# A hybrid mLSTM and attention block on one core: the value product copied out of its bank, with first transfers, last store and fifty pieces at other times

## The chip, the cores and the metric

The kernel runs on one core of one Trainium2 chip, as one launch. The metric is the device time of one execution in microseconds. A core has five engines that each work through their own queue in order: TensorE (PE; its weight loads are shown apart as PEld), VectorE (DVE), ScalarE (ACT), GpSimd (POOL) and SyncE (SP), which only issues transfers here. They meet at semaphores. SBUF holds the tiles, PSUM the eight banks that TensorE writes. Transfers are issued on the queues of SP, ACT and POOL and moved by 16 DMA engines.

## The reference

Sequence of 1024 tokens, model width 1024, float32. One layer:

```python
h = rms(x, norm1_g)
p = h @ w_in
qk_m = silu(dwconv_centred(p[..., C_QK_M:C_V_M], conv_w, conv_b))
mix_a = mlstm_group(qk_m, ...)      # 4 heads x 128, forward and backward scans in chunks of 128
mix_b = diff_attention_group(...)   # 4 heads, q and k of 2 x 64, v of 128, blocks of 128 queries
x = x + concat(mix_a, mix_b) @ w_out
u = square(relu(rms(x, norm2_g) @ w_ff1))      # 4096 wide
x = x + u @ w_ff2
```

In the attention, with two logit matrices per head and a bias by distance:

```python
a = softmax(l0) - lam * softmax(l1)
out = rms(a @ v, sub_g) * (1 - lam_init)
```

## The kernel before

**Matmuls.** A float32 product is made of three passes: each operand is cut into a hi part (rounded to the matmul's format, by a ScalarE copy) and a lo part (the rest, by a VectorE or GpSimd subtract), and hi x hi, lo x hi and hi x lo are summed in PSUM. TensorE's rate over these passes is what the rest is arranged around.

**Stages, in order of time.** The value projection (L207 to L254), with the row norms' squares beside it; the key and gate projection; the query projection and norms of the attention; the conv projections with the depthwise convolution (taps L675) and the mLSTM; the attention with 32 items (8 query blocks, 4 heads), with the out-gate and output projections between them; the MLP's first product, in seven block products per pair of column blocks instead of eight (L1404 to L1406); its second product, likewise (L1733 to L1735).

**The start.** Twelve matmuls on a tile of ones (L196) run while the first transfers are under way. The loop over k takes x tile k and half of a weight tile: SP issues, ScalarE cuts hi (`hhi`, L222, scaled by the norm's vector out of `vecs`), VectorE lo (`hlo`, L223). Of k = 0 the x tile comes in four parts of 256 columns, after the first half of w_v; the 24 matmuls (L237) run hi x hi for all eight token tiles first, then lo x hi, then hi x lo. `wstage` and its `load` (L171 to L174) issue the weight load on SP, cut hi on ScalarE and lo on VectorE.

**The one-hot table.** Four transfers `oh` (L383) feed four matmuls that spread the position bias; three buffers. POOL issues the first three at the start of its queue. The rsqrt of the norms is a power on POOL (L89), with the exponent tile `mhalf` (-0.5).

**Planners.** The order of work on the engines from the conv stage on is written by two planners. Each piece of work has a due time in ticks (a tick is a group of projection matmuls) and a running number; `when` adds it to a table, and `moved` holds by running number what is added to a due time. Where the engines' queues get their order, pieces stand sorted by due time; engines run them in that order. The first table has 956 entries (mLSTM and attention), the second 1160 (MLP).

```python
def when(t, f, *args):
    heapq.heappush(table, (t + moved.get(len(made), 0.0), len(made), f, args))
    made.append(t)
```

**Attention.** An item is one query block of one head. Its steps: both logit products (`att_logits`, L970) into two banks `pl`, with bias and minimum on VectorE (L975); exps on ScalarE (L981); the weighted difference on VectorE (L987 to L990); transposes into `pa` (L997) and copies `at` by ScalarE (L1001); the value product into `pav` (L1008). `pav` is one bank for all items, and also holds the transposes `pt` of four items (L1030). After the product ScalarE squares it with a row sum into `on` (L1014), POOL adds the epsilon and takes the rsqrt (L1015, L1016, L89), VectorE scales `pav` into `on` (L1023). Four items on, `on` is transposed and cut into `mix` (ScalarE L1035, VectorE L1039).

**MLP.** In the first product, `m` banks are read by VectorE (L1487, L1492 and others); weights are cut by ScalarE (L1317) and VectorE (L1320). In the second, step i = 4 is last: `finish` subtracts bank n from `zv[n]` (L1779) and `out` stores it (L1748), n = 0 to 3.

**Head turns.** `head_turn` transposes normalised heads into bank `pzTrue` (L352), cuts them (L128 on ScalarE, L360 on VectorE) into tiles of the tag "zz" and stores them.

Of the kernel before, what the change touches and what calls it, by code (L numbers as in the profile page):

```python
# [10 lines left out]
F32 = mybir.dt.float32  # L11
# [5 lines left out]
P = 128  # L17
# [31 lines left out]
def hybrid_block_kernel(ctx: ExitStack, tc: tile.TileContext, xT, w_v, w_kg, w_c, w_va, w_qa, w_o, w_1, w_2, vec, rel, onehot, outT):  # L49
# [26 lines left out]
    nc.sync.dma_start(vecs[:, 0:V_CW], vec[:, 0:V_CW])  # L76
# [9 lines left out]
    nc.gpsimd.memset(mhalf, -0.5)  # L86

    def rsqrt(out, x, n):
        return nc.gpsimd.tensor_tensor(out, x, mhalf[:, 0:n], op=ALU.pow)  # L89
# [101 lines left out]
    with tc.tile_pool(reuse_waits="tile", name="ps0", bufs=8, space=PSUM) as ps0:  # L191
# [16 lines left out]
        for k in range(KT):  # L208

            parts = (4, 2)[k] if k < 2 else 1  # L210
            n = S // parts
            xts[k] = xt = stp.tile([P, S], F32, tag="xt", name=f"xt{k}", bufs=4)
            if k % 2 == 0:
                whi, wlo, wload = wstage(f"v{k}", nc.vector)
            for i in range(parts):
                sl = slice(i * n, (i + 1) * n)
                if k == 0 and i == 0:
                    wload(w_v[0], 0, HB)
                elif k > 1 and k % 2 == 0:
                    wload(w_v[k // 2], 0, 1024)  # L220
                load = nc.sync.dma_start(xt[:, sl], xT[k][:, sl])
                nc.scalar.activation(hhi[k][:, sl], xt[:, sl], AF.Copy, scale=vcol(V_G1 + k))  # L222
                last = nc.vector.scalar_tensor_tensor(  # L223
                    hlo[k][:, sl], xt[:, sl], vcol(V_G1 + k), hhi[k][:, sl].bitcast(F32), op0=ALU.mult, op1=ALU.subtract
                )
                if k == 0 and i == parts - 1:
                    wload(w_v[0], HB, HB)
            if k > 0:
                squares(k - 1)
            if k > 1:  # L230
                last = add_up(k - 1)
            o = (k % 2) * HB
            ops = [(hhi[k], whi), (hlo[k], whi), (hhi[k], wlo)]
            order = [(t, i) for i in range(3) for t in range(NC)] if k == 0 else [(t, i) for t in range(NC) for i in range(3)]
            for t, i in order:
                a, b = ops[i]
                nc.tensor.matmul(  # L237
                    pv[t], a[:, t * P : (t + 1) * P], b[:, o : o + HB], start=k == 0 and i == 0, stop=k == KT - 1 and i == 2
                )
            if k == 2:  # L240
                with tc.issue_after(load.ins):
                    nc.sync.dma_start(vecs[:, V_CW:], vec[:, V_CW:])
            if k == 5:
                with tc.issue_after(last.ins):
                    parameters()
# [33 lines left out]
    def drain():  # L279
# [91 lines left out]
    def distance_bias():  # L371
# [8 lines left out]
        for i in range(4):  # L380
            sl = slice(i * HB, (i + 1) * HB)
            oh = kgp.tile([32, HB], F32R, tag="oh", name=f"oh{i}", bufs=3)
            nc.gpsimd.dma_start(oh, onehot[:, sl])  # L383
# [7 lines left out]

    def first_norms():
# [4 lines left out]
        rsqrt(rcol, rcol, NC)  # L397
# [12 lines left out]
    for t in range(NC):  # L410
# [33 lines left out]
        if t == 4:  # L444
            pending.append(head_turn(kgp, "zz", 3, zs[0], 0, False))
# [122 lines left out]
    pending.append(head_turn(kgp, "zz", 3, zs[1], 1, False))  # L568
# [3 lines left out]
    def qa_done(t, p):  # L572
        head_norm(kgp, p[:, None, :], (zs[2] if t < 4 else z1)[:, t % 4], t, "q")
        if t == 4:
            pending.append(distance_bias())
            pending.append(head_turn(kgp, "zz", 3, zs[2], 0, True))
# [433 lines left out]
    def att_square(it):  # L1010
# [3 lines left out]
        nc.scalar.activation(it.on, it.pav[:, 0:P], AF.Square, accum_out=sm[:, 5:6])  # L1014
# [6 lines left out]
    def att_unit(it):  # L1021

        nc.vector.tensor_scalar(it.on, it.pav[:, 0:P], it.sm[:, 7:8], None, op0=ALU.mult)  # L1023
# [341 lines left out]
    for j in range(4):  # L1365
# [383 lines left out]

    zx, zv = {}, {}  # L1750
# [32 lines left out]
    for s, (i, j) in enumerate(steps):  # L1783
# [23 lines left out]
        if j == NJ - 1:  # L1807
            for n in range(4):
                f = t + 2.01 + 1.5 + 2 * n if i != 4 else t + 0.5 * (n + 1) + 0.01
                when(f, finish, i, n)  # L1810
# [83 lines left out]
```

## Time and profile before

| | us |
|---|---|
| runs | 1248.34, 1248.34, 1248.42 |
| median | 1248.34 |
| profiled execution, its own time | 1248.9 |
| profiled execution, span | 1247.1 |
| TensorE idle in the span | 12.3 |
| granted TensorE clock | 1.00 |

The page lists busy time per engine, the chain of work that ended last, and groups of instructions by line. In a timeline a row gives the start, the duration, engine, line, operation, what it writes and reads and how many instructions follow one another; in square brackets how long the engine was idle before and which engine and line ended that. A row of the waits names the waiting engine and line, the line it waited for, the sum, the count and the longest. Rows of windows give, per stretch, busy time and instructions of PE, PEld, DVE, ACT and POOL, then the granted clock, the DMA share and GB/s. A matmul of 512 columns is shown with some 0.39 us but the next starts some 0.23 us after it, since they are pipelined.

### The profile page before, as it was taken

Reading aid. Unit: us, or ns where it says so; the run is one execution under the profiler, and the core shown is the slowest. Engines: PE = TensorE matmul, PEld = TensorE weight load, DVE = VectorE, ACT = ScalarE, POOL = GpSimd, SP = SyncE. Lnnn points to the kernel's source line nnn. Section 1 sums busy time; section 2 is a strip of 40 time slices with the busy share of each in tenths; the row PEclk is TensorE's granted clock in tenths of the full one; section 3 lists DMA queues with packets and bytes.
Section 4 is the critical chain, followed back from the end, with each engine's and each line's share of the span. In section 5 each row is a group of like instructions: output and inputs, shape, how many; then the busy total and the mean of one; then the engine's idle time right before and its main releaser. Section 6 shows DMA issues by size and latency. Waiting matters only on the chain.

```text
span 1247.1 us, 17168 instructions
## 1 busy us (share of the span) xinstructions
PE 1234.8 (99%) x6443; PEld 1032.4 (83%) x6443; DVE 824.0 (66%) x1138; ACT 622.1 (50%) x1069; POOL 235.0 (19%) x260
## 2 busy tenths in 40 slices
PE   9999999999999989999999999999999999999998
PEld 7898778888878878888887888888888888888887
DVE  7435558885357787774879886666645774568754
ACT  7223437777446576665456454544534443333332
POOL 0033404464324363422000000000000000004001
PEclk9999999999999999999999999999999999999999
DMA  7404254454275486535544764444359746445732
GB/s 249 152 19 169 45 187 112 112 144 136 82 242 175 158 276 196 166 102 204 176 161 144 269 210 170 156 140 169 134 183 357 265 167 195 136 129 172 223 110 93
DMA packets 101458, 208.31 MB, mean 167 GB/s; under 512 B 8688, under 2 KB 21744, under 8 KB 101376
## 3 DMA queue, kind: packets, MB, share of 16 engines
q1 hardware_dynamic: 78368, 154.50, 38.8%
q10 hardware_dynamic: 15008, 31.50, 6.7%
q0 software_dynamic: 8000, 21.24, 5.3%
q8 instruction: 50, 0.82, 0.3%
q14 instruction: 32, 0.26, 0.1%
HBM read 148.90 MB, written 58.29 MB: 166 GB/s over the span
## 4 chain that ended last, share of the span: by engine, by line
PE 88%; DVE 4%; DMA 2%; POOL 2%; issue 2%; ACT 1%; SPq 0%; ACTq 0%; POOLq 0%; DVEq 0%
PE z L1735 8%; PE z L1733 8%; PE z L1734 8%; PE m L1404 7%; PE m L1405 7%; PE m L1406 7%; PE pav L1008 5%; PE pl L970 4%; PE pv L237 3%; PE pw L138 3%; PE pw L140 2%; PE pw L139 2%; PE pa L997 2%; PE pj_c L138 1%; PE po L138 1%
## 5 line engine op out<-in xcount | busy, mean ns | idle before, releaser
L1771 POOL TENSOR_TENSOR zx<-zx,res 128x512 f32<-128x512 f32 x4 | 8.7, 2179 | 491.5 <-DVE zx L1769 491.5
L1735 PE MATMUL z<-wbh,wa0l 128*128 128x512 f32 x224 | 87.4, 390 | 0.1
L975 DVE CUSTOM_DVE_ANT_0 l<-pl,toe 128x1024 f32<-128x1024 f32 x64 | 76.3, 1222 | 16.7 <-PE pl L970 15.6
L1735 PE MATMUL z<-weh,wa1l 128*128 128x512 f32 x224 | 87.2, 389 | 0.0
L1733 PE MATMUL z<-wbh,wa0h 128*128 128x512 f32 x224 | 87.2, 389 | 0.0
L1734 PE MATMUL z<-wel,wa1h 128*128 128x512 f32 x224 | 87.1, 389 | 0.0
L1734 PE MATMUL z<-wbl,wa0h 128*128 128x512 f32 x224 | 87.1, 389 | 0.0
L1733 PE MATMUL z<-weh,wa1h 128*128 128x512 f32 x224 | 87.1, 389 | 0.0
L1317 ACT ACTIVATE weh<-g 128x1024 fp32r<-128x1024 f32 x28 | 29.7, 1061 | 90.5 <-PE z L1735 53.4
L1317 ACT ACTIVATE wbh<-g 128x1024 fp32r<-128x1024 f32 x28 | 29.7, 1061 | 89.9 <-PE z L1735 53.0
L981 ACT ACTIVATE l<-l,sm 128x1024 f32<-128x1024 f32 x64 | 73.1, 1148 | 1.1 <-DVE sm L975 1.1
L1320 DVE TENSOR_TENSOR wel<-g,weh 128x1024 fp32r<-128x1024 f32 x28 | 35.2, 1258 | 56.8 <-ACT weh L1317 56.8
L1453 ACT ACTIVATE sq<-sq 128x512 f32<-128x512 f32 x48 | 30.3, 630 | 81.5 <-DVE sq L1492 65.4
L1320 DVE TENSOR_TENSOR wbl<-g,wbh 128x1024 fp32r<-128x1024 f32 x28 | 35.4, 1264 | 53.2 <-ACT wbh L1317 53.2
L1008 PEld LDWEIGHTS pav<-v,at 128*128 128x128 f32 x512 | 61.5, 191 | 6.5 <-ACT l L981 1.9
L1008 PE MATMUL pav<-v,at 128*128 128x128 f32 x512 | 62.8, 276 | 2.7 <-DVE on L1023 1.5
L138 PE MATMUL pj_c<-hhi,w_c 128*128 128x512 f32 x128 | 53.3, 417 | 0.0
L970 PE MATMUL pl<-kk,q 64*128 64x512 f32 x384 | 53.3, 409 | 0.0
L138 PE MATMUL pw<-mix,hi_wo 128*128 128x512 f32 x128 | 52.0, 406 | 0.0
L140 PE MATMUL pj_c<-hhi,w_c 128*128 128x512 f32 x128 | 50.4, 394 | 0.0
L1735 PEld LDWEIGHTS z<-wbh,wa0l 128*128 128x128 f32 x224 | 42.1, 188 | 9.7 <-DVE wa0l L1320 0.8
L140 PE MATMUL pw<-mix,lo_wo 128*128 128x512 f32 x128 | 50.0, 391 | 0.0
(454 smaller groups left out, 3606.1 us busy)
## 6 DMA issues: line engine op xcount, KB each, us to landing
g<-g_dram SPq DMA_DIRECT2D x56, 512.0 KB, 4.5
g_dram<-gs SPq DMA_DIRECT2D x64, 256.0 KB, 4.5
g_dram<-sq ACTq DMA_DIRECT2D x42, 256.0 KB, 2.0
kk<-k_dram POOLq DMA_DIRECT2D x16, 512.0 KB, 6.2
raw_wo<-in_w_o_dram SPq DMA_DIRECT2D x16, 512.0 KB, 5.0
re<-in_w_dram SPq DMA_DIRECT2D x16, 512.0 KB, 4.3
ro<-in_w_dram SPq DMA_DIRECT2D x16, 512.0 KB, 3.7
zt<-in_w_dram SPq DMA_DIRECT2D x16, 512.0 KB, 4.3
```

Of the source, the lines that this page charges most:

```text
L138: nc.tensor.matmul(out, ahi, bhi, start=start, stop=False)
L140: latest[0] = nc.tensor.matmul(out, alo, bhi, start=False, stop=stop).ins
L970: nc.tensor.matmul(it.pl[x][:, sl], hd.q[r, i, qi * P : (qi + 1) * P], hd.kk[r, j, sl], start=n == 0, stop=n == 2)
L975: nc.vector.tensor_tensor_reduce(lt, it.pl[m], hd.toe[:, off : off + S], 1.0, 3.0e38, ALU.add, ALU.min, it.sm[:, m : m + 1])
L981: nc.scalar.activation(lt, lt, AF.Exp, bias=sm[:, m : m + 1], scale=-1.0, accum_out=sm[:, 2 + m : 3 + m])
L1008: nc.tensor.matmul(it.pav[:, 0:P], at, it.head.v[:, c], start=c == 0, stop=c == NC - 1)
L1404: nc.tensor.matmul(p, wh, xh, start=go, stop=False, skip_group_check=True)
L1405: nc.tensor.matmul(p, wh, xl, start=False, stop=False, skip_group_check=True)
L1406: nc.tensor.matmul(p, wl, xh, start=False, stop=stop and k == 3, skip_group_check=True)
L1733: nc.tensor.matmul(p, wh, gh, start=go, stop=False, skip_group_check=True)
L1734: nc.tensor.matmul(p, wh, gl, start=False, stop=False, skip_group_check=True)
L1735: nc.tensor.matmul(p, wl, gh, start=False, stop=end, skip_group_check=True)
```

## The change

Six places change.

- **Start.** The first half of w_v is issued on ScalarE's queue and its hi copy made by VectorE; x tile 0 comes in two halves, the norm's vectors behind the first of them, the second half of w_v behind the second (cut by ScalarE). The 24 matmuls of k = 0 go by halves of the token tiles: hi x hi, lo x hi, hi x lo for tiles 0 to 3, then for 4 to 7. `mhalf` is made by ScalarE.
- **One-hot.** The four `oh` issues stand behind the rsqrt of the first row norms on POOL.
- **Head turns.** The tag "zz" has four buffers instead of three.
- **Attention.** ScalarE first copies `pav` into `on` in SBUF; the square reads this copy and writes a tile of its own, `osq` (one buffer); VectorE's scaling reads `on` and writes `on`.
- **Last store.** The last subtract of 128x512 is made in two halves of 256 columns, each stored at once, the first on ScalarE's queue and the second on SP's.
- **Fifty due times,** 33 in the first planner's table and 17 in the second's, are changed or added; many of them change the order on no engine.

```diff
-    nc.sync.dma_start(vecs[:, 0:V_CW], vec[:, 0:V_CW])
...
-    nc.gpsimd.memset(mhalf, -0.5)
...
-            parts = (4, 2)[k] if k < 2 else 1
+            parts = 2 if k < 2 else 1
...
+            if k == 0:
+
+                whi, wlo, raw_v = w_tiles("v0")
+                nc.scalar.dma_start(raw_v[:, 0:HB], w_v[0][:, 0:HB])
+
+                nc.scalar.activation(mhalf, ones[:, 0:16], AF.Copy, scale=-0.5)
+                nc.vector.tensor_copy(whi[:, 0:HB], raw_v[:, 0:HB])
...
+                load = nc.sync.dma_start(xt[:, sl], xT[k][:, sl])
                 if k == 0 and i == 0:
+                    nc.sync.dma_start(vecs[:, 0:V_CW], vec[:, 0:V_CW])
...
+                if k == 0:
+
+                    h = slice(i * HB, (i + 1) * HB)
+                    if i == 1:
+                        nc.sync.dma_start(raw_v[:, h], w_v[0][:, h])
+                        nc.scalar.activation(whi[:, h], raw_v[:, h], AF.Copy)
+                    nc.vector.tensor_tensor(wlo[:, h], raw_v[:, h], whi[:, h].bitcast(F32), op=ALU.subtract)
...
-            order = [(t, i) for i in range(3) for t in range(NC)] if k == 0 else [(t, i) for t in range(NC) for i in range(3)]
+            order = [(t, i) for t in range(NC) for i in range(3)]
+            if k == 0:
+                order = [(t, i) for h in range(2) for i in range(3) for t in range(4 * h, 4 * h + 4)]
...
-            nc.gpsimd.dma_start(oh, onehot[:, sl])
+            with tc.issue_after(rooted[0]):
+                nc.gpsimd.dma_start(oh, onehot[:, sl])
...
-        rsqrt(rcol, rcol, NC)
+        rooted[0] = rsqrt(rcol, rcol, NC).ins
...
-            pending.append(head_turn(kgp, "zz", 3, zs[2], 0, True))
+            pending.append(head_turn(kgp, "zz", 4, zs[2], 0, True))
...
-        nc.scalar.activation(it.on, it.pav[:, 0:P], AF.Square, accum_out=sm[:, 5:6])
+
+        nc.scalar.activation(it.on, it.pav[:, 0:P], AF.Copy)
+        sq = tpool.tile([P, P], F32, tag="osq", name=f"osq{it.qb}{it.h}", bufs=1)
+        nc.scalar.activation(sq, it.on, AF.Square, accum_out=sm[:, 5:6])
...
-        nc.vector.tensor_scalar(it.on, it.pav[:, 0:P], it.sm[:, 7:8], None, op0=ALU.mult)
+        nc.vector.tensor_scalar(it.on, it.on, it.sm[:, 7:8], None, op0=ALU.mult)
...
+    def last_out():
+
+        for q, eng in enumerate((nc.scalar, nc.sync)):
+            sl = slice(q * 256, (q + 1) * 256)
+            nc.vector.tensor_tensor(zv[3][:, sl], zv[3][:, sl], banks[3][:, sl], op=sub)
+            eng.dma_start(outT[7][:, sl], zv[3][:, sl])
...
+                if i == 4 and n == 3:
+                    when(f, last_out)
+                    continue
```

Of the due times, those on which the prediction's steps rest (first table: 35 and 36 are the transposes of a head turn in the conv stage, 583 to 585 square, root and unit of one item of the attention; the second table's 403 to 447 lie about the first blocks of the MLP's first product):

```diff
-        1: 0.691, 20: 0.16, 22: 0.093, 25: -2.784, 36: 4.667, 37: 1.04, 43: -0.133, 92: 2.944, 95: 2.082,
+        1: 0.691, 5: -0.831, 20: 0.16, 22: 0.093, 25: -2.985, 35: 0.788, 36: 6.729, 37: 1.04, 43: -0.133, 52: 0.273,
...
-        576: -0.046, 577: 0.164, 582: 0.308, 583: 0.177, 584: 0.168, 585: 0.062, 586: 0.272, 589: 0.199, 590: 0.004,
+        577: 0.276, 582: 0.308, 583: 0.23, 584: 0.221, 585: 0.114, 586: 0.409, 589: 0.199, 590: 0.141, 592: -0.206,
...
-        147: -0.499, 159: -0.024, 403: 0.444, 404: 0.722, 405: 0.71, 406: 0.304, 417: -0.257, 418: -0.02,
-        446: -0.049, 478: 0.543, 581: 0.182, 600: 0.109, 654: 0.417, 655: 0.138, 656: 0.274, 663: 0.859, 668: 0.021,
+        138: 0.131, 139: -0.54, 147: -0.499, 159: -0.024, 403: 0.38, 404: 0.864, 405: 0.765, 406: 0.353, 407: 0.004,
+        417: -0.257, 418: 0.728, 419: 0.029, 420: 0.02, 436: 0.469, 446: -0.049, 447: -0.63, 464: 0.362, 478: 0.543,
```

More of the change, by code (lines that the diff above doesn't have):

```diff
@@ L208, in hybrid_block_kernel @@
         for k in range(KT):
-            parts = (4, 2)[k] if k < 2 else 1
+            parts = 2 if k < 2 else 1
             n = S // parts
             xts[k] = xt = stp.tile([P, S], F32, tag="xt", name=f"xt{k}", bufs=4)
-            if k % 2 == 0:
+            if k == 0:
[3 more added lines that the diff above has]
+                nc.vector.tensor_copy(whi[:, 0:HB], raw_v[:, 0:HB])
+            elif k % 2 == 0:
                 whi, wlo, wload = wstage(f"v{k}", nc.vector)
+                wload(w_v[k // 2], 0, 1024)
             for i in range(parts):
                 sl = slice(i * n, (i + 1) * n)
+                load = nc.sync.dma_start(xt[:, sl], xT[k][:, sl])
                 if k == 0 and i == 0:
[L218 to L221, printed above, removed]
+                    nc.sync.dma_start(vecs[:, 0:V_CW], vec[:, 0:V_CW])
                 nc.scalar.activation(hhi[k][:, sl], xt[:, sl], AF.Copy, scale=vcol(V_G1 + k))
@@ L225, in hybrid_block_kernel @@
                 )
-                if k == 0 and i == parts - 1:
-                    wload(w_v[0], HB, HB)
+                if k == 0:
[4 more added lines that the diff above has]
+                    nc.vector.tensor_tensor(wlo[:, h], raw_v[:, h], whi[:, h].bitcast(F32), op=ALU.subtract)
             if k > 0:
@@ L390, in distance_bias @@
             yield
+    rooted = [None]
     def first_norms():
@@ L444, in hybrid_block_kernel @@
         if t == 4:
-            pending.append(head_turn(kgp, "zz", 3, zs[0], 0, False))
+            pending.append(head_turn(kgp, "zz", 4, zs[0], 0, False))
     def gates():
@@ L567, in hybrid_block_kernel @@
     norm_end()
-    pending.append(head_turn(kgp, "zz", 3, zs[1], 1, False))
+    pending.append(head_turn(kgp, "zz", 4, zs[1], 1, False))
     pending.append(gates())
```

18 rows, old and new, of the table moved are left out of this document.

## The prediction

> **What bounds the kernel now.** I read the page's busy shares first.
>
> ```profile
> span 1247.1 us, 17168 instructions
> PE 1234.8 (99%) x6443; PEld 1032.4 (83%) x6443; DVE 824.0 (66%) x1138; ACT 622.1 (50%) x1069; POOL 235.0 (19%) x260
> ```
>
> TensorE is idle for 1247.1 - 1234.8 = 12.3 us in all. The change removes no matmul, so it can win only out of these 12.3 us and the slow restarts beside them, while a new wait on TensorE's queue can cost without limit. So I looked in the timeline for each place where TensorE starts late, and asked which of them a part of the change touches. The profiled execution took 1248.9 us, 1.8 above its span and 0.56 above the median of 1248.34; I work the sum against the span and take the same amount off the median.
>
> **Part 1, the first transfers.** Timeline of the first 9 us, the chain there, and the bytes moved in two single microseconds (last figure of a row: GB/s):
>
> ```profile
> 0.72 1.28 ACT L173 ACT_TABLE_LOAD   x1 [0.72 <-PEq L1883]
> 1.12 4.32 PE L196 MATMUL pv<-ones 128*128 128x128 f32 x24 [1.12 <-POOL ones L74]
> 1.16 0.42 SPq L171 DMA_DIRECT2D raw_v<-in_w_v_dram  x1
> 3.98 0.63 ACT L173 ACTIVATE w_v<-raw_v 128x512 fp32r<-128x512 f32 x1 [1.98 <-DMA raw_v<-in_w_v_dram]
> 5.20 0.70 PE L237 MATMUL pv<-w_v,hhi 128*128 128x512 f32 x2
> 6.34 0.73 PE L237 MATMUL pv<-w_v,hhi 128*128 128x512 f32 x2 [0.44 <-ACT hhi L222]
> 7.42 1.20 PE L237 MATMUL pv<-w_v,hhi 128*128 128x512 f32 x4 [0.34 <-ACT hhi L222]
> 7.42 42.92 PE pv L237 x188
> 2.00:3.00 1.00, 1.00 (x7) 1.00 (x7) 0.00 (x0) 0.00 (x1) 0.99 (x3) 1.00 0.63 176
> 3.00:4.00 1.00, 1.00 (x6) 1.00 (x6) 0.00 (x0) 0.02 (x1) 0.40 (x1) 1.00 1.05 333
> L222 ACT ACTIVATE hhi<-xt,vecs x6: 493/508/726, 4.5 to 9.8; 128x256 fp32r<-128x256 f32 x4, 128x512 fp32r<-128x512 f32 x2
> L223 DVE SCALAR_TENSOR_TENSOR hlo<-xt,vecs,hhi 128x512 fp32r<-128x512 f32 x2 | 1.4, 750 | 0.7 <-ACT hhi L222 0.7
> L174 DVE TENSOR_TENSOR w_v<-raw_v,w_v 128x512 fp32r<-128x512 f32 x2 | 1.4, 692 | 4.9 <-ACT w_v L173 4.9
> ```
>
> The chain's 188 matmuls at an unbroken pace cost 42.92/188 = 0.228 each. The first two start at 5.20 and should be followed at 5.66; the next pair comes at 6.34 (0.68 late). That pair should be followed at 6.80; the next four come at 7.42 (0.62 late). Together 1.3 us, and 0.1 more until the pace holds: **1.4 us** is what a perfect start would give back. It cannot be more than about 0.2 above that, because the warm-up matmuls of L196, which the change keeps, hold TensorE until 1.12 + 4.32, or about 5.2 where the first L237 overlaps them.
>
> After the change the two things that the first block needs, half of w_v (256 KB) and half of x tile 0 (256 KB), are issued side by side on two queues when these begin (0.72 in the first row), instead of one after the other on SP. The two window rows sum to 509 KB by 4.0, so both halves have landed at about 4.0 to 4.2. ScalarE's hi cut of 512 columns (0.73 at most) ends near 4.9, before 5.2. VectorE meanwhile makes the hi copy of the weights (at most the 0.69 of its subtract), then hlo (0.75) to 5.65 and wlo (0.69) to 6.35. TensorE's new order wants hlo after four matmuls (5.2 + 0.9 = 6.1) and wlo at 7.0, then the second half of x at 7.9. That half is the next 256 KB, at 176 to 333 GB/s 0.8 to 1.5 us behind the first: landed by 5.7, cut by 6.4. All are in time. I take **-1.4**; bounds -1.0 (the cut ends 0.4 after 5.2) and -1.6. vecs, which the hi cut also needs, now travels behind the x half; it is a few columns only, inside the 4.0 to 4.2.
>
> One rule says where this might fail. The row above has the table load at 0.72, at the head of ScalarE's queue though its ACTIVATE waits until 3.98. The Trainium skill (ScalarE: Activation LUTs, section "Table sets: the hidden batching unit") says that the compiler puts a load before every activation that needs one: by that it would come behind the new DMA issue and cost nothing. If it stays at the head, raw_v is issued at 2.0 and not at 0.7; this is a rival below, priced from the rows.
>
> **Part 2, one tick in the conv stage.** Timeline of TensorE at 174 us, and what it waited for:
>
> ```profile
> 174.29 0.39 PE L140 MATMUL pj_c<-hhi,w_c 128*128 128x512 f32 x1
> 174.82 0.66 PE L352 MATMUL pzTrue<-ident,z 128*128 128x128 f32 x4
> PEld pzTrue L352 <- DVE zzTrue L360: 0.6, 1, 0.6
> ```
>
> The transposes of the next head should start at 174.52 and start at 174.82, since their bank is still read. Entry 35 moves them one tick (six matmuls, 1.4 us) later: **-0.3**, bounds 0 and -0.3. The third buffer more of "zz" and the moved exps, taps, sums and gates of this planner pass sit on VectorE and ScalarE where TensorE shows no late start; the one-hot issues move to POOL's empty time behind the rsqrt. I cost these at 0: the cover is TensorE's own queue of projections. Without it a late 128x1024 tap would show, so bounds of plus and minus 0.4.
>
> **Part 3, the copy of the value product.** Two stretches differ. Rows: windows with sums by engine (PE, PEld, DVE, ACT, POOL), then the timeline.
>
> ```profile
> 400.00:425.00 25.00, 25.00 (x171) 20.58 (x170) 17.19 (x31) 16.83 (x36) 9.93 (x19) 1.00 0.48 143
> 439.00:466.00 27.00, 23.87 (x193) 19.61 (x189) 22.98 (x42) 21.23 (x46) 16.79 (x25) 1.00 0.80 283
> L1014 ACT ACTIVATE on<-pav x32: 257/278/285, 378.5 to 588.3; 128x128 f32<-128x128 f32 x32
> L1001 ACT ACTIVATE at<-pa x64: 582/596/600, 371.8 to 582.6; 128x512 f32<-128x512 f32 x64
>   PEld pav L1008: 0.8, 1
> 446.00 0.26 ACT L1014 ACTIVATE on<-pav 128x128 f32<-128x128 f32 x1
> 446.84 1.09 ACT L1001 ACTIVATE at<-pa 128x512 f32<-128x512 f32 x2 [0.49 <-PE pa L997]
> 447.32 1.11 POOL L1015 TENSOR_SCALAR sm<-sm 128x1 f32<-128x1 f32 x1
> 448.79 0.56 POOL L89 TENSOR_TENSOR sm<-sm,mhalf 128x1 f32<-128x1 f32 x1
> 449.38 0.35 DVE L1023 TENSOR_SCALAR on<-pav,sm 128x128 f32<-128x128 f32 x1 [1.08 <-POOL sm L89]
> 449.88 2.02 PE L1008 MATMUL pav<-v,at 128*128 128x128 f32 x16 [1.54 <-DVE on L1023]
> 452.71 1.66 PE L970 MATMUL pl<-kk,q 64*128 64x512 f32 x12
> 454.81 0.66 PE L1030 MATMUL pt<-ident,on 128*128 128x128 f32 x4 [0.45 <-DVE on L1023]
> 459.38 1.05 ACT L128 ACTIVATE hi_wo<-raw_wo 128x1024 fp32r<-128x1024 f32 x1
> 461.04 2.02 PE L1008 MATMUL pav<-v,at 128*128 128x128 f32 x16 [0.38 <-ACT at L1001]
> ```
>
> Most items are filled with projection matmuls: TensorE is busy all 25 us of the first window and the copy must only not hurt. It adds one PSUM read of 128x128 to ScalarE per item, 0.28 by L1014's row, 32 x 0.28 = 9 us on an engine with 25 - 16.83 = 8.2 us free in that window, which holds not four items (32 in 588.3 - 378.5, 6.6 us each), so about 1 us more. Queued behind it are the square, the exps and the `at` copies, for which TensorE waited once in 64. So 0 in the filled items.
>
> In 439 to 466 the filling is missing: 27 - 23.87 = 3.1 us of idle TensorE. Now the product at 449.88 waits for its bank, which frees when VectorE's scaling ends at 449.73, and that waits for POOL's rsqrt. With the copy, the bank is free about 446.3 (446.00 + 0.26) and the product can start at 448.3, behind its `at` copies (446.84 + 1.09, and the copy's 0.28 ahead of them): 1.5 us earlier. But the next thing of that queue is the following item's logits at 452.71, which need VectorE's logit passes to free both `pl` banks; those passes are paced by VectorE (22.98 of 27 busy), and only the 0.35 plus 0.1 of the scaling in front of them moves away. So I count 0.4 of the 1.5 there. Next, square and rsqrt of that item come 1.5 us earlier, so the four transposes at 454.81 no longer wait for the scaling (0.45 idle); they then wait for the logits' own end: 0.4; the next product follows them through VectorE's `mix` and comes as much earlier, without a gain of its own. At 461.04 the `at` copy stands behind a 1.05 us weight cut on ScalarE; the moved square, root and unit (583 to 585) put the cut ahead of the square, which gives 0.2 more of the 0.38. Sum **-1.0**; bounds -0.3 (POOL's 1.11 us passes or VectorE hold the pace anyway) and -1.6.
>
> **Part 4, the MLP's order.** TensorE and VectorE at 703 us:
>
> ```profile
> 702.54 0.69 DVE L1320 TENSOR_TENSOR wbl<-re3b,wbh 128x512 fp32r<-128x512 f32 x1 [0.75 <-ACT wbh L1317]
> 703.15 0.68 DVE L1492 TENSOR_TENSOR sq<-w,m 128x512 f32<-128x512 f32 x1
> 703.39 0.39 PE L1406 MATMUL m<-x3h,wbl 128*128 128x512 f32 x1
> 703.89 0.50 PE L1404 MATMUL m<-x4h,wd0h 128*128 128x512 f32 x1
> 704.22 0.39 PE L1405 MATMUL m<-x4l,wd0h 128*128 128x512 f32 x1
> ```
>
> Two matmuls should take 0.45 and take 704.22 - 703.39 = 0.83: 0.4 late, since L1492 frees the bank behind a cut for which VectorE idled 0.75. The moved entry puts the bank's reader into that idle time: **-0.4**, bounds 0 and -0.4. Other moves of this table exchange neighbours on VectorE at 0.
>
> **Part 5, the last store.**
>
> ```profile
> 1243.51 0.69 DVE L1779 TENSOR_TENSOR zv<-zv,z 128x512 f32<-128x512 f32 x1 [0.67 <-PE z L1735]
> 1244.22 0.33 SPq L1748 DMA_DIRECT2D out_dram<-zv  x1
> ```
>
> Today 1243.51 + 0.69 + 0.02, then issue and 256 KB to the end at 1247.1. Split, the first half is ready near 1243.95 and the second near 1244.4 (0.2 later than now, for the fixed part of a second instruction), but only 128 KB are left to move; at the 333 GB/s seen above that is 0.4 instead of 0.8. -0.4 + 0.2 = -0.2, with the second queue's free issue slot **-0.3**; bounds 0 and -0.4.
>
> **Sum:** -1.4 - 0.3 - 1.0 - 0.4 - 0.3 = -3.4. Span 1243.7, profiled execution 1245.5, median 1248.34 - 3.4 = **1245.0**.
>
> **Rivals.**
> 1. The attention stretch does not move: POOL's chain (1.11 + 0.56 per item) and VectorE set the pace, parts 2 and 4 give half. -1.4 - 0.3 - 0.3 - 0.3 = -2.3: 1246.0. For it: 22.98 of 27 busy on VectorE. Against: the scaling itself is part of that pace.
> 2. The start gives nothing. With the table load at the head, raw_v is issued at 2.0; at the 3.98 - 1.16 = 2.8 us of today it lands at 4.8, the copy (0.69) ends at 5.5, 0.3 late. That alone costs 0.3 of the 1.4; nothing is left only if the x half comes late too (the sum is then -2.0: 1246.3).
> 3. Other late starts go as well, of which I count none: more of the 12.3 us, another 1.7 or so: 1243.3.
> 4. Slower: the copy stands on TensorE's chain in the filled items. ScalarE takes its queue in order; if the `at` copies of the next item stand behind copy and square with less than 0.28 us to spare, each of some 26 filled items (32 less six about the unfilled stretch and the ends) is 0.28 longer: +7.3, less the 2.4 of the other parts, +4.9: 1253.2. For it: 9 us of new work on ScalarE. Against: 8.2 free microseconds in 25, and one wait in 64 for those copies.
>
> **How the numbers follow.** Forecast 0.62, rival 1 0.19, rival 2 0.08, rival 3 0.06, rival 4 0.05. A measurement tells apart about 0.2%, 2.5 us: faster means below 1245.84. The forecast's own range is 1244.0 to 1245.8; with rivals 1 to 3 and the bounds of the parts (-5.0 at the best, -1.1 at the worst without rival 4) the range is 1242.9 to 1247.2, and rival 4 stays outside. Faster 0.62 + 0.06 = 0.68, same 0.19 + 0.08 = 0.27, slower 0.05.
>
> **What the profile would show.** Right: L237 unbroken from 5.2, ending 1.4 earlier; no idle TensorE before L352 at about 173; between 435 and 465 no wait of the product for L1023, and idle TensorE there down from 3.1 to about 2; the two L1404 and L1405 after 703 without their 0.4; the last store's end 2.6 us or less after the last subtract's begin. Wrong: hhi or raw_v landing after 4.6; TensorE waiting for the `at` copies item after item; POOL's L89 later than now.

## The result: slower by 0.25%

| | before | changed |
|---|---|---|
| median, us (15 executions each) | 1248.44 | 1252.15 |
| lowest to highest, us | 1248.19 to 1249.92 | 1249.19 to 1254.23 |
| profiled execution: own time, span, us | 1248.9, 1247.1 | 1250.89, 1249.1 |
| ratio to before, 95% interval | | 1.0025 [1.0018, 1.0032] |

Forecast were 1245.0 and a range of 1242.9 to 1247.2. Two things stand in the table: the profiled execution is 2.0 us longer than that of before, and most other executions of the changed kernel are longer still. The first has a cause that the runs show; for the second the runs show a cause in a sister kernel, and that it is the same here is inferred.

The first rows of the page after:

```profile
span 1249.1 us, 17148 instructions
PE 1236.8 (99%) x6443; PEld 1035.0 (83%) x6443; DVE 838.5 (67%) x1138; ACT 626.1 (50%) x1097; POOL 238.6 (19%) x259
L1043 DVE TENSOR_SCALAR on<-on,sm 128x128 f32<-128x128 f32 x32 | 24.3, 760 | 38.7 <-POOL sm L87 25.8
```

TensorE's idle time is still 12.3 us (1249.1 - 1236.8), but that total hides a shift, as the stages below show. The surprise is the third row, from the list of groups: VectorE's scaling, 351 ns from PSUM before, takes 760 ns on the mean, though it now reads SBUF. VectorE is 14.5 us busier (838.5 - 824.0), nearly all of it here: 32 x (0.760 - 0.351) = 13.1.

To see where the time goes I read the start of the same matmul in both timelines, at the ends of the stages, and subtracted (us; changed minus before):

| stage that ends there | at (before) | difference | of the stage |
|---|---|---|---|
| value projection | 47.2 | +0.14 | +0.14 |
| projections, conv and mLSTM | 301.5 | +0.42 | +0.28 |
| attention, filled items | 434.5 | +0.48 | +0.06 |
| product in the unfilled stretch | 461.0 | -0.19 | -0.67 |
| logits behind it | 464.2 | +1.84 | +2.03 |
| attention's end, out projection | 617.9 | +2.35 | +0.51 |
| first part of the MLP | 716.0 | +2.02 | -0.33 |
| end of the span | 1247.1 | +2.0 | 0.0 |

Almost all of it comes within 3 us, from 461 to 464. TensorE's idle time moved the same way: between the starts at 434.5 and 461 it fell from 3.1 to 1.6 us, and in the 3 us behind it rose from 0 to 1.8. That the two totals agree is chance. Timeline of VectorE, GpSimd and TensorE there, first before, then in the changed kernel:

```profile
460.51 2.37 POOL L1091 TENSOR_TENSOR lo_wo<-raw_wo,hi_wo 128x1024 fp32r<-128x1024 f32 x1
460.55 0.35 DVE L1023 TENSOR_SCALAR on<-pav,sm 128x128 f32<-128x128 f32 x1 [0.72 <-POOL sm L89]
461.03 1.22 DVE L975 CUSTOM_DVE_ANT_0 l<-pl,toe 128x1024 f32<-128x1024 f32 x1
463.87 1.65 PE L970 MATMUL pl<-kk,q 64*128 64x512 f32 x12
```

```profile
460.50 0.56 POOL L87 TENSOR_TENSOR sm<-sm,mhalf 128x1 f32<-128x1 f32 x1
460.85 2.05 PE L1025 MATMUL pav<-v,at 128*128 128x128 f32 x16
461.04 2.35 POOL L1111 TENSOR_TENSOR lo_wo<-raw_wo,hi_wo 128x1024 fp32r<-128x1024 f32 x1
461.10 2.38 DVE L1043 TENSOR_SCALAR on<-on,sm 128x128 f32<-128x128 f32 x1 [1.02 <-POOL sm L87]
463.61 1.23 DVE L992 CUSTOM_DVE_ANT_0 l<-pl,toe 128x1024 f32<-128x1024 f32 x1
464.89 0.50 PE L987 MATMUL pl<-kk,q 64*128 64x512 f32 x1 [1.12 <-DVE sm L992]
```

In the changed kernel GpSimd ends the rsqrt at 461.06 and begins at once with its next piece, a weight subtract of 2.35 us. The rsqrt also releases VectorE's scaling. The scaling begins 0.06 us after the subtract and ends 0.09 us after it (463.48 against 463.39). The logit pass behind it on VectorE, and then TensorE's next logits, come 2 us late. Of the 32 scalings seven take about 2.4 us; each of the seven runs beside a weight subtract of GpSimd and ends with it, the other 25 take 0.285 to 0.40. In the kernel before the same seven stand beside the same subtracts, read PSUM and take 0.35. Only the one at 461 costs TensorE 2 us: the one near 395 lies in the filled items, and from 464 to 618, where the other five stand, the whole loss is 0.51.

### The profile page after: what moved, and what is told of

Same layout as the page of the kernel before. It is cut to its first block, busy times and chain, and to the rows that moved or that the text cites. A ratio compares the mean times of both kernels' runs of the same rounds, so it can differ in the third digit from the quotient of the medians.

```text
span 1249.1 us, 17148 instructions
## 1 busy us (share of the span) xinstructions
PE 1236.8 (99%) x6443; PEld 1035.0 (83%) x6443; DVE 838.5 (67%) x1138; ACT 626.1 (50%) x1097; POOL 238.6 (19%) x259
## 4 chain that ended last, share of the span: by engine, by line
PE 89%; DVE 5%; DMA 1%; ACT 1%; POOL 1%; issue 1%; ACTq 0%; DVEq 0%; SPq 0%; POOLq 0%
PE z L1756 8%; PE z L1755 8%; PE z L1754 8%; PE m L1425 7%; PE m L1426 7%; PE m L1427 7%; PE pav L1025 4%; PE pv L248 4%; PE pl L987 3%; PE pw L136 2%; PE pw L138 2%; PE pw L137 2%; PE pa L1014 2%; PE po L136 1%; PE pkg L136 1%
## 5 line engine op out<-in xcount | busy, mean ns | idle before, releaser
L992 DVE CUSTOM_DVE_ANT_0 l<-pl,toe 128x1024 f32<-128x1024 f32 x64 | 76.3, 1221 | 8.1 <-PE pl L987 6.0
L1337 ACT ACTIVATE wbh<-g 128x1024 fp32r<-128x1024 f32 x28 | 29.7, 1061 | 90.5 <-PE z L1756 53.0
L1337 ACT ACTIVATE weh<-g 128x1024 fp32r<-128x1024 f32 x28 | 29.7, 1061 | 89.9 <-PE z L1756 53.4
L1043 DVE TENSOR_SCALAR on<-on,sm 128x128 f32<-128x128 f32 x32 | 24.3, 760 | 38.7 <-POOL sm L87 25.8
```

The lines of the kernel that those rows point to most:

```text
L992: nc.vector.tensor_tensor_reduce(lt, it.pl[m], hd.toe[:, off : off + S], 1.0, 3.0e38, ALU.add, ALU.min, it.sm[:, m : m + 1])
```

## Experiments

Fourteen kernels ran beside the two. Where a table gives start differences they are read as above, against the profiled execution of before.

### Which part of the change

**The attention alone** (e1): the three lines of the attention part, in the kernel before.

```diff
-        nc.scalar.activation(it.on, it.pav[:, 0:P], AF.Square, accum_out=sm[:, 5:6])
+        nc.scalar.activation(it.on, it.pav[:, 0:P], AF.Copy)
+        nc.scalar.activation(sq, it.on, AF.Square, accum_out=sm[:, 5:6])
...
-        nc.vector.tensor_scalar(it.on, it.pav[:, 0:P], it.sm[:, 7:8], None, op0=ALU.mult)
+        nc.vector.tensor_scalar(it.on, it.on, it.sm[:, 7:8], None, op0=ALU.mult)
```

> The kernel before with the attention part alone (copy, square and scaling on the copy; due times as before). Theory, shared SBUF access: VectorE's scaling from SBUF stands still while GpSimd runs a 128x1024 weight subtract, so a few of the 32 scalings take about 2.4 us where all took 0.35 from PSUM, and one of them in the unfilled stretch near 461 us holds TensorE some 2 us: 1249.5 to 1252.5. Rival, the due times do it: scalings may be long, but the time is within 0.5 of 1248.4 or below it. Rival, ScalarE's copy does it: slower, with all scalings near 0.29 us.

**Everything but the attention** (e2): the same lines undone in the changed kernel.

> The changed kernel without its attention part (square and scaling from PSUM as before), all else as changed. Shared SBUF access: scalings all at 0.35 us, no hold of about 2 us near 465, time 1247.5 to 1249.3, some 3 below the changed kernel. Rival, the due times: it stays at 1251 to 1252.5.

**The scaling on GpSimd** (e3), with the copy kept:

```diff
         rsqrt(it.sm[:, 7:8], it.sm[:, 7:8], 1)
+        nc.gpsimd.tensor_scalar(it.on, it.on, it.sm[:, 7:8], None, op0=ALU.mult)
...
-        nc.vector.tensor_scalar(it.on, it.on, it.sm[:, 7:8], None, op0=ALU.mult)
+        pass
```

> The changed kernel with the scaling on GpSimd, right behind its rsqrt, instead of on VectorE. ScalarE's copy and all due times stay. Shared SBUF access: no VectorE instruction of this place is left to be held, so the 1.1 us holds of the logits near 465 go; 1247 to 1249.5. Rival, ScalarE's copy and its queue: no gain, 1251 to 1252.5.

**The out weights' subtracts on VectorE** (e4): `split_ahead(..., w_o[n], nc.vector, t, "O")` for `nc.gpsimd`.

> The changed kernel with the eight weight subtracts 128x1024 of the first half's out projection on VectorE instead of GpSimd. Shared SBUF access: of the seven scalings near 2.4 us those beside these subtracts go to 0.29 to 0.4 us (the one near 395 is beside a weight subtract of the gates and may stay); time 1248 to 1250.5, with some VectorE time (1.25 us each) given back. Rival: a scaling of 2.4 us has its own reason, the durations stay.

| | median | ratio to before | at 434 | at 461 | at 464 | at 500 | at 1233 |
|---|---|---|---|---|---|---|---|
| e1 | 1250.63 | 1.0014 [1.0005, 1.0024] | +0.97 | +0.90 | +2.29 | +2.67 | +2.33 |
| e2 | 1248.19 | 0.9998 [0.9988, 1.0007] | -0.68 | -0.69 | -0.69 | -0.67 | -0.84 |
| e3 | 1248.98 | 1.0000 [0.9991, 1.0009] | -0.93 | -1.16 | -0.93 | +0.06 | +0.02 |
| e4 | 1250.05 | 1.0006 [0.9996, 1.0016] | +0.13 | +0.37 | +1.67 | +1.98 | +1.76 |

The attention part is the loss: with it alone the kernel is slower, without it the rest is level with before, and between 434 and 500 e1 loses 1.70, e2 nothing. In e1, with the old due times, the scaling at 461 is held as well:

```profile
461.47 2.46 DVE L1026 TENSOR_SCALAR on<-on,sm 128x128 f32<-128x128 f32 x1 [1.03 <-POOL sm L89]
```

In e4 the seven long scalings become one, the one near 395, whose neighbour is a weight subtract of the gates, which stayed on GpSimd: the held scaling hangs on GpSimd's subtract and on nothing of its own. But e4's total says nothing for the theory: the subtract itself, 1.22 us, now stands on VectorE ahead of the logit pass, and e4 loses 1.30 between 461 and 464 for that. e3 keeps the copy and loses only 0.23 there, then 1.0 between 464 and 476: the logit passes wait for GpSimd's scaling (L992, 8.0 us in six waits).

**Six statistics buffers** (e5): e3 with `bufs=6` for the tag "sm", since GpSimd is now the last to read it.

> As the run with the scaling on GpSimd, with six buffers of the row statistics (sm) instead of four. In that run VectorE's logit passes waited 1.74 and 1.17 us for GpSimd's scaling about 461 and 466 us, and TensorE lost 1.0 us between 464 and 476. If this wait is for the statistics' buffer that GpSimd now reads last, it goes and the time is 1247.0 to 1248.4, below the kernel before. Rival: GpSimd's chain itself sets the pace, the loss stays, 1248.4 to 1249.8.

**The copy kept, the scaling from PSUM** (e6):

```diff
-        nc.vector.tensor_scalar(it.on, it.on, it.sm[:, 7:8], None, op0=ALU.mult)
+        nc.vector.tensor_scalar(it.on, it.pav[:, 0:P], it.sm[:, 7:8], None, op0=ALU.mult)
```

> The changed kernel with ScalarE's copy and the square on the copy kept, but VectorE's scaling reading PSUM as before. Shared SBUF access: all scalings 0.35 us, none near 2.4; no loss of TensorE of about 2 us near 464, 1247.5 to 1249.3. Rival, the added copy on ScalarE's queue: 1250.5 or more as in the changed kernel.

e5: 1248.29 (0.9997 [0.9987, 1.0007]); the waits for GpSimd's scaling go. e6: 1250.04 (1.0009 [1.0000, 1.0019]), against my number. All its scalings are at 0.349 to 0.353, as expected, and there is no step of 2 us; but it loses 0.3 to 0.8 at each of the items from 443 to 461, 1.65 from 434 to 500. Here the bank is again freed only by the scaling, and copy and square now lie one behind the other in front of it. So e6 doesn't part the two theories. Its rows fit a copy that costs where the chain from product to freed bank runs through it, and those of e5 a copy that wins where the bank is freed by it: e5's logits of 452.71 come at -2.59, 1.7 earlier than its own -0.88 before.

### The start

**Eight warm-up matmuls** (e7): `range(8)` for `range(12)` in the changed kernel. **The start alone** (e8): the start part in the kernel before.

> The changed kernel with 8 instead of 12 warm-up matmuls. Theory of the start: TensorE's rate doubles at a moment that differs from run to run (4.05 to 6.2 us so far), and twelve warm-ups at the slow rate end at 6.2 instead of 5.2, after the first block's hi cut (5.25). With eight they end by 4.6; the first block starts near 5.25 in every run and the k = 1 block 0.3 to 0.8 us earlier than the 12.23 of the changed kernel where the rate doubles late. Rival: the first block is bound by its transfers, k = 1 starts at 12.1 or later. The attention is that of the changed kernel: scalings of 2.4 us where GpSimd's weight subtracts run, whole time 1249 to 1253.

> The kernel before with the start alone (first transfers, halves, order of the first 24 matmuls). Prediction on record: 1.4 faster, 1247.0. Theory now: 1.3 faster only where the rate doubles by about 4 us, 0.4 to 0.9 where it doubles at 5 to 6 us: 1247.2 to 1248.2. Rival: no gain in any run, 1248.3 to 1249.

e7: 1253.64 (1.0039 [1.0024, 1.0054]); e8: 1248.38 (0.9995 [0.9985, 1.0004]). e7 is slower, and e8's gain over its own before, 0.3 us on the medians, lies inside its interval. The theory behind e7 fell. Timeline of TensorE's start in the changed kernel and in e7:

```profile
1.12 5.49 PE L194 MATMUL pv<-ones 128*128 128x128 f32 x24 [1.12 <-POOL ones L74]
6.27 1.59 PE L248 MATMUL pv<-w_v,hhi 128*128 128x512 f32 x4
```

```profile
5.44 2.08 PE L248 MATMUL pv<-w_v,hhi 128*128 128x512 f32 x4 [0.54 <-ACT hhi L226]
7.31 1.91 PE L248 MATMUL pv<-w_v,hlo 128*128 128x512 f32 x4
```

The warm-ups start 0.213 us apart and, once the rate has doubled, 0.112. In the profile of before 13 of the 23 steps from one start to the next are slow, up to 4.05; in the changed kernel all are, to 6.2, so that the first block waits for warm-ups, not for its hi cut, which ends at 5.25 (L226 at 4.53, 0.72 long). In e1, whose start is that of before line for line, the rate doubles at 5.8 and the k = 1 block begins at 12.60 instead of 12.09. Over the thirteen profiles of the new start with twelve warm-ups that block begins between 11.04 and 12.23, 11.57 on the mean; the only two of the old start, before and e1, give 12.09 and 12.60. With eight warm-ups TensorE pauses 0.54 us, the rate has not doubled by the end of the first half of the block (matmuls 0.43 apart), and k = 1 begins at 13.38: in this one profile the pause costs more than the shorter warm-up wins. The Trainium skill (TensorE: Matmul & The Clock Gate, "What's actually happening") says that the rate follows a free-running window of activity and that the number of slow matmuls differs from run to run; these profiles agree on the number: 13 to 23 of 23 steps.

### What lifts the other executions

**The subtract later** (e9): two due times more in the changed kernel, `338: 0.945` (first out weight's subtract) and `119: 0.3545` (MLP's c22(0)).

> The changed kernel with two due times more: the first out weight's subtract on GpSimd (338) goes behind the next head's loads instead of right behind the rsqrt of the item near 461 us, and the MLP's c22(0) (119) goes ahead of the sum it had been put behind. Theory: the scaling near 461 is 0.29 us instead of 2.4, TensorE loses under 0.4 us between the product at 461 and the logits at 464 (2.0 in the changed kernel), and about 676 TensorE idles some 0.9 us instead of 1.5; whole time 1248.3 to 1250.0, 2 to 3.5 below the changed kernel, since shorter idle times also let the granted clock fall less often. Rival, VectorE's own work holds the logits near 464: the loss stays, 1251 or more.

e9: 1253.41 (1.0030 [1.0020, 1.0040]), far from what I expected, though the scaling near 463 is 0.29. Timeline of ScalarE and TensorE in e9, then windows of 2 us (third last figure: granted clock):

```profile
457.31 0.58 ACT L1018 ACTIVATE at<-pa 128x512 f32<-128x512 f32 x1
460.55 1.06 ACT L126 ACTIVATE hi_wo<-raw_wo 128x1024 fp32r<-128x1024 f32 x1 [2.65 <-DMA raw_wo<-in_w_o_dram]
462.11 0.58 ACT L1018 ACTIVATE at<-pa 128x512 f32<-128x512 f32 x1
462.74 2.70 PE L1025 MATMUL pav<-v,at 128*128 128x128 f32 x16 [1.84 <-ACT at L1018]
```

```profile
462.00:464.00 2.00, 1.26 (x11) 1.26 (x12) 0.65 (x2) 2.00 (x6) 1.11 (x3) 0.99 1.06 409
464.00:466.00 2.00, 2.00 (x12) 2.00 (x11) 2.00 (x5) 1.45 (x5) 0.00 (x0) 0.50 0.87 329
466.00:468.00 2.00, 2.00 (x12) 1.55 (x12) 1.64 (x5) 1.60 (x5) 1.59 (x2) 0.66 0.22 80
```

The change moved the square of this item (583) behind the cut of the first out weight (337). The `at` copy stood behind the cut before, too; but ScalarE now comes to the cut earlier, in the changed kernel's profile at 457.80 where it was 459.38 before. ScalarE works in order. The weight is issued at 451.8, and in this execution it lands 2.65 us after ScalarE could use it; the `at` copy comes late, TensorE idles 1.84 us, and then runs at half clock for some 3.4 us. From 457 to 464 this costs 3.1 us. In the profiled execution of the changed kernel the same weight, issued at 451.69, was there when ScalarE came to it, at 457.80; in e4 ScalarE waited 1.77 us for it.

How long this weight takes from issue to landing separates the sixteen profiles: 4.7 to 4.8 us in the five kernels in which the scaling frees the bank (before, e2, e6, e8, e11), 5.0 to 8.7 in the eleven in which the copy does. Why is not shown: the next head's loads on GpSimd are issued 1.2 us behind this weight in the changed kernel and in e9, and 2.0 before, but that does not order the eleven. e2 and e11 have the same order on ScalarE, and no execution of theirs is above 1250.0. In e1, with the old order, the weight lands 7.9 us after its issue and ScalarE does not wait; in e4, with the new order, 7.8 us mean a wait of 1.77. So order and landing count together.

**The cut later too** (e12): e9 with `337: 0.53`, which puts the cut behind the `at` copy and two exps. Nothing else differs.

> The run lo_later (1253.41) with one due time more: ScalarE's cut of the first out weight (337) goes behind the at copy and two exps that it stood ahead of. Theory: what lifts lo_later and many executions of the changed kernel is ScalarE standing still for this weight's landing, with the fall of the clock that follows TensorE's idle time; so TensorE idles under 0.6 us at the product near 461, no window between 455 and 470 shows a clock below 1.00, 1248.3 to 1249.8, 3.5 to 5 below lo_later. Rival, GpSimd's and VectorE's chain is the bound there: 1251 or more.

e12: 1250.06 (1.0010 [1.0001, 1.0020]), 3.35 below e9, and its ten executions lie in 1248.98 to 1251.21 where e9's nine lie in 1249.97 to 1253.94. No window of the profile shows a lower clock, and from 434 to 464 it gains 0.52 (-0.66 to -1.18). So the late weight in ScalarE's queue is what lifts e9, by far the larger part of it. From 461 to 464, where the changed kernel loses 2.03, e12 loses 0.03: copy and scaling from SBUF are there, and no subtract runs beside this scaling (0.29). My number was a little too good, for the hold came back one item later:

```profile
471.81 2.35 POOL L1111 TENSOR_TENSOR lo_wo<-raw_wo,hi_wo 128x1024 fp32r<-128x1024 f32 x1
471.87 2.38 DVE L1043 TENSOR_SCALAR on<-on,sm 128x128 f32<-128x128 f32 x1 [1.08 <-POOL sm L87]
476.83 1.43 PE L987 MATMUL pl<-kk,q 64*128 64x512 f32 x10 [0.65 <-DVE sm L992]
```

The second out weight's subtract meets the scaling as the first did before. Between 464 and 500 e12 loses 2.34 (-1.18 to +1.16), 1.15 of it between 470 and 476, behind this hold. Most of the rest is lost by 470. There another row stands out: VectorE's update of the logits beside the first out weight's subtract, which now runs from 467.30 to 469.69.

```profile
468.53 2.25 DVE L1007 SCALAR_TENSOR_TENSOR l<-l,sm,l 128x1024 f32<-128x1024 f32 x1
```

One item earlier the same update takes 1.28. So a subtract that is moved off the scaling can hold VectorE's next instruction with two SBUF inputs instead; that this is the 0.85 lost by 470 is argued from the rows (a like pair, with the order turned round, stands under part 2 below).

### Can the copy win

**No attention part, c22(0) ahead** (e11): e2 with one due time of the MLP. **GpSimd relieved** (e10): e5 with that due time and one subtract of the gates on VectorE. **Cut and subtract later** (e13): e5 with that due time and two of the attention. **Three parts only** (e14): the kernel before with the changed start, the copy with the scaling on GpSimd and six buffers, and the MLP's changed due times with c22(0) ahead; the conv's and the attention's due times and the last store stay as before.

```diff
e10, e11, e13, e14
-        15: 0.182, 117: 0.641, 118: 0.463, 119: 0.434, 120: 0.135,
+        15: 0.182, 117: 0.641, 118: 0.463, 119: 0.3545, 120: 0.135,
e10
-            nc.gpsimd.tensor_tensor(mm[:, 1], V["so"], mm[:, 0].bitcast(F32), op=ALU.subtract)
+            nc.vector.tensor_tensor(mm[:, 1], V["so"], mm[:, 0].bitcast(F32), op=ALU.subtract)
e13
-         226: 0.157, 283: -0.65, 333: 0.296, 334: 0.011, 541: 0.285,
+         226: 0.157, 283: -0.65, 333: 0.296, 334: 0.011, 337: 0.53, 338: 0.6, 541: 0.285,
```

> The changed kernel without the attention part (run before: 1248.19) and with c22(0) ahead again. The wait of TensorE about 676 us is 0.9 instead of 1.5 us: 0.6 less in that stretch, 0.3 to 0.6 in all: 1247.5 to 1248.0. Rival: what is won at 676 is lost by 704, where the changed order had won 0.4; 1248.2.

> Scaling on GpSimd with six statistics buffers (run before: 1248.29), and now the gate's last subtract on VectorE instead of GpSimd and c22(0) ahead again. In that run GpSimd was late with the last scaling of the group at 454.03, TensorE idled 1.67 us there and the granted clock then fell to 0.5 for about 3 us. With 2.3 us of subtract off GpSimd before it, TensorE waits under 0.5 us at those transposes, the clock holds, and the time is 1246.0 to 1247.5, below both kernels. Rival: another piece of GpSimd's queue (the loads of the next head) is late instead; 1248 to 1249.

> Scaling on GpSimd with six statistics buffers (1248.29), the same later cut and subtract of the first out weight, c22(0) ahead again. Theory: the copy wins up to 1.7 us by 452 as in that run; the transposes at 454 may still wait for GpSimd (1.67 us idle there) but ScalarE's queue no longer stops: 1247.0 to 1248.3. Rival: nothing gained over 1248.3, since GpSimd is the bound.

> Kernel before with three parts only: the start, the copy with the scaling on GpSimd (six statistics buffers), and the MLP's due times with c22(0) ahead; first planner table, one-hot, head turns and last store as before. From the stage differences: start -0.9, first table 0 instead of +0.2, attention -0.2 to -1.0, MLP -0.1 to -0.3: 1246.5 to 1247.8, below both kernels. Rival: the attention loses with the old due times what it wins, 1248.0 to 1249.0.

| | median | ratio to before | at 434 | at 461 | at 500 | at 1233 |
|---|---|---|---|---|---|---|
| e5 | 1248.29 | 0.9997 [0.9987, 1.0007] | -0.88 | -0.50 | -0.65 | -0.68 |
| e10 | 1248.62 | 0.9995 [0.9985, 1.0005] | +0.44 | +0.07 | -0.08 | -0.43 |
| e11 | 1248.17 | 0.9991 [0.9982, 1.0001] | -0.24 | -0.25 | -0.24 | -0.38 |
| e13 | 1247.22 | 0.9988 [0.9978, 0.9998] | -0.44 | -2.46 | -1.72 | -1.80 |
| e14 | 1247.03 | 0.9990 [0.9981, 1.0000] | -1.34 | -1.24 | -1.42 | -1.40 |

e13 beats both kernels, that of before by 1.6 us on the medians with an interval that only just clears 1; e14's reaches 1. In e13, with VectorE out of the scaling and ScalarE's queue not stopped, the copy wins 2.0 us by 461, of which 0.7 is lost again by 500 (its transposes near 475 wait for GpSimd). e10 missed its number: the last scaling on GpSimd is late all the same (TensorE idles 0.56 us at 455), and logits wait for VectorE at 448. e11 is level with before within its interval, as its rival had it: at 676 TensorE idles 0.98 instead of 1.63 in e2, but 0.52 is lost again at 678, where TensorE waits for VectorE's L1337, and from there on both win alike, 0.4 by 680 and 0.4 at 703. From 666 to 716 e11 wins 0.08 and e2 0.15, so the one due time moved the loss by 2 us and won nothing. e14 has the start's gain; in the attention its transposes wait 1.66 us for GpSimd, and it ends level there.

## Why the prediction was wrong, step by step

**Part 3, the copy: the sign was wrong.** The mechanism that I counted on is there: the product no longer waits for the scaling, and by 461 the changed kernel has gained 0.67 in this stretch, within my bounds of -0.3 to -1.6. The step that failed is the one that took the scaling's new place as free: "only the 0.35 plus 0.1 of the scaling in front of them moves away". I looked at what the copy adds to ScalarE, and not at what reading SBUF instead of PSUM exposes VectorE to. The scaling took 2.38 instead of 0.35, and +2.03 stood against -0.67. That the hold makes this step is shown for these 3 us (e6, e12); no run keeps copy and scaling on VectorE and has no hold in the whole stretch to 500, so how the rest of the loss divides stays open. The Trainium skill has the rule (GPSIMD Engine Reference, section "Specifications"): GpSimd's SBUF interfaces are shared with VectorE, with contention for VectorE's instructions in a two-port mode or with two SBUF inputs. The traces agree for the scaling: 2.4 us beside a subtract, 0.35 in all 32 from PSUM beside the same subtracts (before, e6). Which of the page's two conditions the scaling meets no run shows. Without a collision the scaling is indeed faster from SBUF, 0.289 against 0.351.

The second failure in this part: "the moved square, root and unit (583 to 585) put the cut ahead of the square, which gives 0.2 more". I priced the move by its order and took the weight's landing for granted. ScalarE now comes sooner to a transfer that the copy lets land later, in front of TensorE's next operand; where it lands late, 3.1 us go (e9). That this lifts e9 is shown, since e9 and e12 differ in this order alone. The changed kernel's own long executions left no trace, so that for them it is inferred.

**Rival 4** named ScalarE as the engine that the copy could put on the chain, but in the filled items. There nothing happens: +0.06 from 301 to 434. The slower outcome came by a mechanism that I had not listed.

**Part 1, the start: a term was mis-sized.** In the changed kernel's profile no matmul of the first block waits for an operand. What failed first is "hold TensorE until 1.12 + 4.32, or about 5.2": one execution's value taken as a constant. What failed second is "inside the 4.0 to 4.2" for `vecs`. ScalarE waits for it, and the hi cut ends at 5.25, not at 4.9:

```profile
4.53 0.72 ACT L226 ACTIVATE hhi<-xt,vecs 128x512 fp32r<-128x512 f32 x1 [1.85 <-DMA vecs<-in_vec_dram]
```

So even where the rate doubles early the first block begins at 5.49 to 5.61 (e8, e6, e5), and the best start on record is worth 1.05 (e8: k = 1 at 11.04), not 1.4. With 11.57 instead of 12.09 to 12.60 for the k = 1 block, the new start is worth 0.5 to 1.0 on the mean; in the one profiled pair it lost 0.14. Rival 2's condition did not occur: the table load stands behind the issue (1.17).

**Part 2, the conv stage: right where I looked, given back elsewhere.** The 0.3 before L352 is gone, as is a wait at 158 (0.2). But at 201 there is a new one. VectorE in that stretch, before and after, and GpSimd and TensorE after:

```profile
195.43 4.43 DVE L675 SCALAR_TENSOR_TENSOR q<-pad,vecs,q 128x1024 f32<-128x1024 f32 x3
```

```profile
195.06 6.41 DVE L692 SCALAR_TENSOR_TENSOR q<-pad,vecs,q 128x1024 f32<-128x1024 f32 x3
197.85 2.54 POOL L645 TENSOR_TENSOR w_c<-raw_c,w_c 128x1024 fp32r<-128x1024 f32 x1 [0.81 <-ACT w_c L126]
201.79 0.60 PE L766 MATMUL pd<-va,kt 128*128 128x129 f32 x3 [0.53 <-DVE st L775]
```

The three taps take 6.41 instead of 4.43: a weight subtract of GpSimd fell beside them, and the state update behind them came late for TensorE. It costs 0.68 in the changed kernel, and 0.5 to 0.7 in ten more of the profiles with the new due times; e1, e8 and e14, with the old ones, don't have it. I had put this at 0 with bounds of 0.4. The one exception is e7. There the subtract comes later, 0.17 us behind the begin of the third tap (198.61), and it is the subtract that is held:

```profile
195.98 3.92 DVE L692 SCALAR_TENSOR_TENSOR q<-pad,vecs,q 128x1024 f32<-128x1024 f32 x3
198.78 3.38 POOL L645 TENSOR_TENSOR w_c<-raw_c,w_c 128x1024 fp32r<-128x1024 f32 x1 [5.29 <-ACT w_c L126]
```

In the eleven profiles with the step the subtract begins before the third tap or with it, and this tap takes 3.3 to 3.5 us; in e7, e1 and e14 the tap begins first and takes 1.3 to 1.5, and the subtract takes 3.3 to 3.4 instead of 2.4. So the one that begins first holds the other. No run was made for this, but the fourteen profiles in which the two meet agree. (Near a tie the scaling lost: at 515.61 in the changed kernel it began 0.03 us ahead of a subtract and took 2.51 all the same.)

**Part 4, the MLP: the step came, the agreement of the total is luck.** -0.33 against -0.4. The wait at 703 went, as forecast, and gave 0.40; but c22(0) behind a sum cost 0.56 at 676, and 0.5 came back by 680, neither of which I had listed. This stretch also moves without any change in it: e1 and e8 have the MLP of before, and from 618 to 716 e1 gains 0.50 (0.40 of it at 703, where TensorE comes later) and e8 loses 0.66.

**Part 5, the last store: nothing.** Timeline at the end, changed kernel:

```profile
1245.51 0.75 DVE L1775 TENSOR_TENSOR zv<-zv,z 128x256 f32<-128x256 f32 x2 [0.67 <-PE z L1756]
1246.33 0.33 SPq L1776 DMA_DIRECT2D out_dram<-zv  x1
```

The second half is issued 0.82 after the subtracts begin (before: 1244.22 - 1243.51 = 0.71), and from there to the end of the span it is 2.8 (1249.1 - 1246.33) where 256 KB took 2.9. Half the bytes save 0.1, not the 0.4 that I had from a rate: of these 2.9 us nearly all stays when the size is halved. From the begin of the last subtract to the end it is 3.6 in both kernels.

**The sums.** The parts' own bounds add up to -4.7 and -0.9, not to -5.0 and -1.1, and the low end of 1242.9 follows from neither. The last sign, 2.6 us from subtract to end, does not fit a term of -0.3 either, since the rows before give 3.6. None of this decides anything: 1252.15 lies far above every version.

## What to carry to other kernels

Moving an operand from PSUM to SBUF changes which neighbours can hold its reader: look up what GpSimd runs right then, above all when the same event releases both; of two that collide, the one that begins clearly first holds the other. An engine that works in order turns a transfer's landing into the wait of everything behind it, so price a move by the latest landing and not by the one in the trace (4.7 us before, up to 8.7 with the copy). A start-up term that depends on the clock needs several profiles before it becomes a number in a sum.

## What the runs showed of the hardware

After the start, the granted clock falls behind an idle spell of TensorE, at times. In the sixteen profiles of this case no spell under 1.65 us was followed by a lower clock, among them six of 1.54 to 1.56 (before at 449.88 is one). Of the six spells from 1.66 to 1.85 us three were: 1.67 in e5, 1.84 in e9, 1.85 in e7. The clock went to 0.50 for about 3.4 us, at a price of some 1.5 us: e7's eight matmuls came 0.43 apart instead of 0.23. Windows of one microsecond behind the 1.67 us spell in e5:

```profile
454.00:455.00 1.00, 0.91 (x7) 0.91 (x8) 0.00 (x0) 0.55 (x1) 1.00 (x3) 0.83 1.12 420
455.00:456.00 1.00, 0.79 (x5) 0.39 (x3) 0.82 (x2) 1.00 (x2) 1.00 (x3) 0.50 1.00 394
457.00:458.00 1.00, 1.00 (x6) 1.00 (x6) 0.93 (x5) 0.82 (x1) 0.00 (x0) 0.50 1.12 397
458.00:459.00 1.00, 1.00 (x11) 0.88 (x9) 0.77 (x1) 0.23 (x1) 0.00 (x0) 0.96 1.11 401
```

So a wait of 1.7 us can cost 3. The Trainium skill (TensorE: Matmul & The Clock Gate, "Why this matters for your kernels") warns of idle gaps above some 3 us; here about half of that was enough.
